# A hybrid decoder layer: projection evacuations at the recurrent chain's rank, and attention tiles taken narrow and wide by turns

## The chip, the cores and the metric

The kernel runs on one core of one Trainium2 chip. Each engine (TensorE or PE, VectorE or DVE, ScalarE or ACT, GpSimd or POOL, SyncE or SP) works through its own queue in order; semaphores order work between them. The metric is device time in microseconds (us) for one execution of the whole layer. Times are given for the median of several runs; the profile shows one execution of its own.

## The reference

The layer has a model width of 1024 and a sequence of 1024 tokens, batch 1, all float32. It computes two mixers side by side from one input projection, then an MLP:

```python
h = _rms_norm(x, norm_mix_pre[i])
z = h @ w_in_first                       # one combined projection
q, k, v = z[..., 0:512], z[..., 512:1024], z[..., 1024:1536]
zs = _token_shift(z[..., 1536:...], mu_shift[i])   # z + (prev - z) * mu
r_r, k_r, v_r = zs[..., 0:512], zs[..., 512:1024], zs[..., 1024:1536]
attn = _rms_norm(_dilated_attention(q, k, v), attn_out_gain[i])
rw = _rwkv7(r_r, k_r, v_r, xw, xa, xg, ...)        # a recurrence over the tokens
x = x + _rms_norm(jnp.concatenate([attn, rw], -1) @ w_out[i], norm_mix_post[i])
h = _rms_norm(x, norm_ffn_pre[i])
x = x + _rms_norm(jnp.square(jax.nn.relu(h @ w_ffn_up[i])) @ w_ffn_down[i], norm_ffn_post[i])
```

The attention has 8 heads of 64. It is causal, with three dilated branches combined by their softmax denominators; this is the same as one softmax over all earlier keys with the logarithm of a count (how many branches contain the distance) added to the score. The other mixer, RWKV-7, has 8 heads of 64 and a 64x64 state per head, updated token by token.

## The kernel before

**Stages.** Until about 47 us the input is loaded, normalised and transposed, and the first low-rank (LoRA) columns are projected. From 47 to 477 us TensorE does 24 projections of 128 columns each, named `k0`..`k3`, `r0`..`r3`, `v0`..`v3` (for RWKV, one for each pair of heads) and `aq0`..`av3` (queries, keys, values of the attention). Between them it does the RWKV work: for each pair of heads a preparation (`pre_pair`: products `kk`, `ar`, `bk`, `km`, and a matrix `pN`), a triangular inversion on VectorE (`subst`: many small `tmp`, `Zt` steps), its merge (`merge`: `X`, `Z`, `qu`), and then, from about 320 to 455 us, a serial chain over eight blocks of 128 tokens. From 477 to 626 us the attention runs, then the mixing with `w_out` until about 717 us, then the MLP until the end at 1346 us.

**A projection.** It takes two halves of 512 tokens, each in one PSUM bank of the tag `z` (two banks). Each half is 8 steps of three matmuls (a product of split operands in fp32r). After the last step `ev` (in `proj_spill`) evacuates the bank. For RWKV columns that is `shift_evac`: ScalarE writes the bank times 1 − mu (line 198), VectorE keeps the last column times mu as a carry (200) or adds that carry (202), and adds the bank shifted by one token times mu (203). For `aq` and `ak` ScalarE writes a rounded copy and VectorE the remainder, and both go to DRAM (`qk_d`); for `av` ScalarE copies and stores to `zs_d`. Only when the evacuation has read the bank can the next half but one start in it.

**What sets the order.** The queues of TensorE and SP are written out by hand: `drive` interleaves the steps of the projections and of the RWKV jobs by a simulated clock (a job's step yields its cost; due times come from a table), and from the attention on TensorE's order is the order of the code. VectorE, ScalarE and GpSimd are ordered by a scheduler with priorities: `tc.high_priority(offset=n)` lets what is written inside go earlier by n places than where it stands. `PRI = (300, 600, 3500, 2500)`: the preparation and its norms run at 300, `subst`, `merge` and parts of the chain's blocks at 600, the serial steps of the chain at 3500, the attention at 2500. The projections' steps have no such offset.

**The attention.** It runs over 4 pairs of heads, 8 query tiles i of 128 tokens and 2 heads h, 64 steps m in all. A tile i has 128(i+1) keys, so tiles 0 to 3 fit one bank of 512 (narrow here) and 4 to 7 need two (wide). For each step, `at_s` does the scores `pS` (two matmuls for each bank), VectorE adds the penalty strip `stripT` and takes the minimum (894), and ScalarE takes the exp and its sum (896). `at_t` transposes the exps on TensorE into PSUM (`pT`, 906): the first four blocks into bank `a`, copied out by ScalarE (908), the others into bank `c`, copied out by VectorE (910), both into the tile `PT`. `at_s` runs two steps ahead of `at_t`. `at_v` multiplies with the values (`po`) after every second tile. After tiles 3 and 7 it divides (`ao`, 928), stores to `a_d`, squares on ScalarE (`sqa`, 933) and reduces on VectorE (`sq`, 934). `at_vt` transposes the next pair's values (`vt`, 875 and `Vt`, 876). `load_wo` prepares parts of `w_out` (`WO`, 945, 946) without an offset.

**The start of the attention.** SP's queue issues the loads of `qs`, `kh`, `kl` (865), of the values `vT` (870) and of `stripT` (853), in an order that follows from the scheduled program.

Of the kernel before, what the change touches and what calls it, by code (L numbers as in the profile page):

```python
# [8 lines left out]
F32 = mybir.dt.float32  # L9
# [8 lines left out]
P = 128  # L18
# [22 lines left out]
def hybrid_kernel(tc, x, par, cst, strip, win, wup_lora, gup, gnwb, grow, wout, wup, wdown, out, dbg=None):  # L41
# [7 lines left out]
    def mm_h(o, lhsT, rhs, start=True, stop=True):  # L49

        for s_ in range(2):
            last = mm(o[64 * s_:64 * s_ + 64], lhsT[:, 64 * s_:64 * s_ + 64], rhs, start, stop)
        return last
# [10 lines left out]
    with (  # L64
# [658 lines left out]
        def slabs(todo, done):  # L723

            def pick():
                j = next((j for j, t in enumerate(todo) if t[3] is None or t[3] in done), None)
                if j is None:
                    return None
                u = todo.pop(j)
                raw, hi_, lo_ = load_w(wslab(2 + u[1]), u[0], A)  # L730
                for q in (slice(0, 4), slice(4, 8)):
                    V.tensor_tensor(lo_[:, q], raw[:, q], hi_[:, q].bitcast(F32), OP.subtract)
                return u, hi_, lo_

            nxt = None
            while todo or nxt:
                nxt = nxt or pick()
                if not nxt:
                    yield None
                    continue  # L740
                (nm, i, shift, _), hi_, lo_ = nxt
                nxt = pick()
                ev = proj_spill(nm, i, shift)
                for hf in range(2):
                    pz = ps.tile([P, 512], F32, name=f"z_{nm}_{hf}", tag="z")
                    ts = slice(hf * 512, hf * 512 + 512)
                    for k in range(KB):
                        mm3(pz, hi_[:, k, :], lo_[:, k, :], hT[:, 0, k, ts], hT[:, 1, k, ts], k == 0, k == KB - 1)
                        if k == KB - 1:
                            ev(hf, pz)  # L750
                        yield 0.7, [f"{nm}_{hf}", nm][:1 + hf] if k == KB - 1 else []

        def drive(todo, jobs):
# [99 lines left out]
        nc.sync.dma_start(stripT, strip)  # L853

        at, sx, pts, pos, aset = {}, {}, {}, {}, {0: ap_}

        def at_load(p):

# [19 lines left out]
        def at_s(p, i, h):  # L878

            QS, KH, KL = at[p]  # L880
            w = P * (i + 1)
            if i == 0 and h == 0:
                at[p, "den"] = sm.tile([P, 8, 2], F32, name=f"den{p}", tag="den")
                at[p, "rden"] = sm.tile([P, 8, 2], F32, name=f"rden{p}", tag="rden")
            Sx = sx[p, i, h] = ap_.tile([P, S], F32, name=f"S{p}_{i}_{h}", tag="Sx", bufs=3)
            mn = sm.tile([P, 2], F32, name=f"mn{p}_{i}_{h}", tag="mn", bufs=4)
            nbk = 1 if w <= 512 else 2
            for k in range(nbk):
                lo, hi = 512 * k, min(w, 512 * k + 512)
                pS = ps.tile([P, 512], F32, name=f"pS{p}_{i}_{h}_{k}", tag="wz"[k if i > 3 else h] if p > 0 or i > 4 else "w")  # L890
                for q in range(2):
                    mm(pS[:, :hi - lo], QS[h][:, i * P:(i + 1) * P], (KH, KL)[q][h][:, lo:hi], q == 0, q == 1)
                so = S - w + lo
                V.tensor_tensor_reduce(Sx[:, lo:hi], pS[:, :hi - lo], stripT[:, so:so + hi - lo], 1.0,  # L894
                                       3e38 if k == 0 else mn[:, 0:1], OP.add, OP.min, accum_out=mn[:, k:k + 1])
            A.activation(Sx[:, :w], Sx[:, :w], AF.Exp, scale=-1.0, bias=mn[:, nbk - 1:nbk], accum_out=at[p, "den"][:, i, h:h + 1])  # L896
# [14 lines left out]

        def at_v(p, i0):

            Vt, qg = at[p, "v"], i0 // 4
            if i0 % 4 == 0:
                pos[p, qg] = ps.tile([P, 4, 2, 64], F32, name=f"po{p}_{qg}", tag="by"[qg], bufs=1)
            po = pos[p, qg]
            for i in (i0, i0 + 1):
                for h in range(2):
                    PT = pts.pop((p, i, h))  # L920
                    for j in range(i + 1):
                        mm_h(po[:, i % 4, h], PT[:, j], Vt[:, j, h * 64:h * 64 + 64], j == 0, j == i)
            if i0 % 4 == 0:
                return
            rden = at[p, "rden"][:, 4 * qg:4 * qg + 4]
            V.reciprocal(rden, at[p, "den"][:, 4 * qg:4 * qg + 4])
            ao = ap_.tile([P, 4, 2, 64], F32, name=f"ao{p}_{qg}", tag="ao", bufs=1)
# [153 lines left out]
        for _ in range(LEAD):  # L1081
            next(rest, None)
        hi_pri = lambda: tc.high_priority(offset=PRI[3])
        step = lambda m: (m // 16, m % 16 // 2, m % 2)
        with hi_pri():
            at_load(0)
            at_s(*step(0))
            at_s(*step(1))
        for m in range(64):
            p, i, h = step(m)  # L1090
            with hi_pri():
                if m + 2 < 64:
                    at_s(*step(m + 2))
                at_t(p, i, h)
                if h == 1 and i % 2 == 0 and m > 1:
                    at_v(*((p, i - 2) if i else (p - 1, 6)))
                if h == 1 and i == 0:
                    at_vt(p)
                if m == 17 or m == 33:
                    at_load(p + 1)  # L1100
# [411 lines left out]
```

## Time and profile before

| | us |
|---|---|
| median of 3 runs | 1355.21 |
| lowest and highest run | 1354.86, 1359.75 |
| the profiled execution's own time | 1348.41 |
| its span in the profile | 1346.3 |
| VectorE busy | 903.5 |
| ScalarE busy | 624.8 |

The profiled execution is 6.8 us below the median of the runs. The span leaves out 2.1 us around the first and last instruction. A row of waits gives the engine and the line that waited, then who released it, the sum in us, how often, and the longest. A row of a timeline gives the start in us, the duration of one, the engine, the line, the operation, its output and inputs, and in brackets how long the engine had stood and who released it. In such rows names have lost their numbers: `z_v` is any half of any of the `v` projections. A window's row gives its bounds, its length, busy time and count of PE, weight loads, DVE, ACT and POOL, the clock granted to TensorE (1.00 is full), the DMA engines' busy share and GB/s.

### The profile page before, as it was taken

The page shows a single profiled execution, that of the slowest core. Times are in us where ns is not written, and L with a number is a line of the kernel's source. Part 1 is how long each engine was busy: PE and PEld are TensorE (multiplying, and loading weights), DVE is VectorE, ACT ScalarE, POOL GpSimd, SP SyncE. Part 2 cuts the span into 40 slices and gives each one's busy share as a digit, 9 for nine tenths or more (in the row PEclk, how much of TensorE's full clock was granted, in tenths as well). Part 3 has the DMA queues.
Part 4 walks back from the last instruction along what each step waited for, and adds up shares of the span by engine and source line. Part 5 has one row for each costly group of instructions (what it writes and reads, how often), then busy time and mean ns, then how long its engine had stood idle before and what let it go on. Part 6 is the DMA issues. An engine that isn't in the chain of part 4 may idle for free.

```text
span 1346.3 us, 23565 instructions
## 1 busy us (share of the span) xinstructions
PE 1280.9 (95%) x9360; PEld 1056.4 (78%) x9360; DVE 903.5 (67%) x1647; ACT 624.8 (46%) x1026; POOL 36.2 (3%) x56
## 2 busy tenths in 40 slices
PE   6999999899999988999998999999999999999997
PEld 5777888787777867787886788888888888888875
DVE  7867657632678556555889977667766776456587
ACT  7652324223455366665647444343444344443442
POOL 0000000000000000000000000000000002000210
PEclk9999999999999999999999999999999999999999
DMA  7346746778686587602434454454467985345564
GB/s 257 115 172 165 196 119 187 196 217 240 168 255 190 168 271 186 168 17 87 139 112 141 164 168 137 157 172 148 138 199 232 344 332 160 105 135 194 188 206 168
DMA packets 163757, 239.48 MB, mean 178 GB/s; under 512 B 52192, under 2 KB 89312, under 8 KB 163648
## 3 DMA queue, kind: packets, MB, share of 16 engines
q1 hardware_dynamic: 154304, 212.81, 50.5%
q10 hardware_dynamic: 8064, 20.98, 4.7%
q0 software_dynamic: 1280, 4.20, 0.8%
q8 instruction: 73, 1.20, 0.4%
q14 instruction: 36, 0.29, 0.1%
HBM read 160.85 MB, written 77.09 MB: 177 GB/s over the span
## 4 chain that ended last, share of the span: by engine, by line
PE 72%; DVE 12%; DMA 8%; ACT 4%; issue 3%; SPq 1%; DVEq 0%; ACTq 0%
PE X L47 12%; PE dX L47 9%; PE Z L47 6%; PE pm L47 6%; PE dZ L47 5%; PE dY L47 3%; PE z_v L47 3%; PE z_aq L47 3%; PE Y L47 3%; PE z_k L47 3%; DMA bv<-v_d 2%; PE po L47 2%; PE pT L906 2%; PE z_av L47 2%; PE z_r L47 2%
## 5 line engine op out<-in xcount | busy, mean ns | idle before, releaser
L47 PE MATMUL dX<-wow,wou 128*128 128x512 f32 x768 | 175.9, 390 | 2.4 <-DVE wow L1173 1.9
L47 PEld LDWEIGHTS dX<-wow,wou 128*128 128x128 f32 x768 | 143.8, 188 | 33.8 <-DVE wow L1173 3.2
L47 PE MATMUL dZ<-wow,wou 128*128 128x512 f32 x384 | 87.4, 389 | 0.0
L47 PEld LDWEIGHTS dZ<-wow,wou 128*128 128x128 f32 x384 | 72.1, 188 | 15.0
L1172 ACT ACTIVATE wow<-wd 128x1024 fp32r<-128x1024 f32 x40 | 42.3, 1060 | 88.6 <-PE dZ L47 29.8
L1173 DVE TENSOR_TENSOR wou<-ur,wou 128x1024 fp32r<-128x1024 f32 x56 | 72.0, 1287 | 7.3 <-ACT wou L1172 7.1
L1173 DVE TENSOR_TENSOR wow<-wd,wow 128x1024 fp32r<-128x1024 f32 x40 | 49.9, 1250 | 34.5 <-ACT wow L1172 33.9
L1172 ACT ACTIVATE wou<-ur 128x1024 fp32r<-128x1024 f32 x56 | 58.5, 1048 | 20.7 <-DMA ur<-u_d 13.3
L894 DVE CUSTOM_DVE_ANT_0 S<-pS,stripT 128x512 f32<-128x512 f32 (+3 forms) x64 | 37.5, 588 | 33.9 <-PE pS L47 19.5
L896 ACT ACTIVATE S<-S,mn 128x128 f32<-128x128 f32 (+7 forms) x64 | 49.4, 772 | 17.3 <-DVE mn L894 17.1
L1260 ACT ACTIVATE r<-u 128x512 f32<-128x512 f32 x48 | 30.0, 626 | 52.1 <-DVE u L1258 51.9
L906 PE MATMUL pT<-cst,S 128*128 128x128 f32 x288 | 44.7, 279 | 8.7 <-DVE PT L910 4.2
L47 PE MATMUL z_aq<-hT,wh_aq 128*128 128x512 f32 x128 | 47.3, 424 | 3.5 <-DVE ev_v L203 3.5
L47 PE MATMUL pm<-WO,mxr 128*128 128x512 f32 x192 | 49.4, 400 | 1.0 <-DVE mn L894 0.7
L1173 DVE TENSOR_TENSOR wow<-TK,wow 128x1024 fp32r<-128x1024 f32 x16 | 20.8, 1301 | 38.9 <-ACT wow L1172 38.9
L906 PEld LDWEIGHTS pT<-cst,S 128*128 128x128 f32 x288 | 32.3, 140 | 17.9 <-ACT PT L908 6.7
L47 PE MATMUL Z<-HB,wo 128*128 128x512 f32 x192 | 46.1, 389 | 0.0
L47 PE MATMUL pm<-WO,mxa 128*128 128x512 f32 x192 | 45.8, 394 | 0.0
L47 PE MATMUL z_k<-hT,wh_k 128*128 128x512 f32 x128 | 44.0, 405 | 1.7 <-DVE z L234 1.4
L47 PE MATMUL z_av<-hT,wh_av 128*128 128x512 f32 x128 | 45.3, 408 | 0.0
L47 PE MATMUL X<-HB,wo 128*128 128x512 f32 x180 | 43.7, 390 | 1.6 <-ACT HB L1034 1.6
L47 PE MATMUL z_v<-hT,wh_v 128*128 128x512 f32 x128 | 42.9, 400 | 1.0 <-DVE ev_r L203 1.0
(388 smaller groups left out, 3056.1 us busy)
## 6 DMA issues: line engine op xcount, KB each, us to landing
ur<-u_d SPq DMA_DIRECT2D x56, 512.0 KB, 4.4
wd<-in_wdown_dram SPq DMA_DIRECT2D x40, 512.0 KB, 4.2
u_d<-S SPq DMA_DIRECT2D x64, 256.0 KB, 2.1
u_d<-u SPq DMA_DIRECT2D x48, 256.0 KB, 2.2
wr_upa<-in_wup_dram SPq DMA_DIRECT2D x16, 512.0 KB, 3.6
wr_upb<-in_wup_dram SPq DMA_DIRECT2D x16, 512.0 KB, 4.0
TK<-in_wdown_dram SPq DMA_DIRECT2D x16, 512.0 KB, 7.4
x<-in_x_dram SPq DMA_DIRECT2D x8, 512.0 KB, 6.9
```

Source lines behind the costliest of these rows:

```text
L47: return PE.matmul(o, lhsT, rhs, start=start, stop=stop, skip_group_check=True)
L894: V.tensor_tensor_reduce(Sx[:, lo:hi], pS[:, :hi - lo], stripT[:, so:so + hi - lo], 1.0, 3e38 if k == 0 else mn[:, 0:1], OP.add, OP.min, a ...
L896: A.activation(Sx[:, :w], Sx[:, :w], AF.Exp, scale=-1.0, bias=mn[:, nbk - 1:nbk], accum_out=at[p, "den"][:, i, h:h + 1])
L906: PE.transpose(pt[:, j], Sx[:, (4 * k + j) * P:(4 * k + j + 1) * P], ident)
L1172: A.activation(w[:, 0, 0:n], raw, AF.Copy)
L1173: E.tensor_tensor(w[:, 1, 0:n], raw, w[:, 0, 0:n].bitcast(F32), OP.subtract)
L1260: A.activation(r, src, AF.Relu)
```

## The change

The change has three parts. First, the evacuation of each projection is written inside the offset `PRI[2]`, 3500, that of the chain's serial steps. Second, the attention takes its query tiles in the order `TO`, 0, 4, 1, 5, 2, 6, 3, 7, so that a narrow and a wide tile come by turns. With it, the scores of a narrow tile always use banks of the tag `w`, and of a wide tile `w` and `z`; before, the second head's narrow tiles used `z`. In pair 0 the first five tiles of the new order use `w` alone, since the last projection still holds `z`. Third, both `po` banks are taken at a pair's start, and division, store and square move into `at_out`, called for both halves at the end of a pair. The line numbers after the change differ by 1 before the attention and by 2 to 4 in it.

```diff
--- before.py
+++ after.py
@@ -747,7 +747,8 @@
                     for k in range(KB):
                         mm3(pz, hi_[:, k, :], lo_[:, k, :], hT[:, 0, k, ts], hT[:, 1, k, ts], k == 0, k == KB - 1)
                         if k == KB - 1:
-                            ev(hf, pz)
+                            with tc.high_priority(offset=PRI[2]):
+                                ev(hf, pz)
                         yield 0.7, [f"{nm}_{hf}", nm][:1 + hf] if k == KB - 1 else []
@@ -853,6 +854,7 @@
         at, sx, pts, pos, aset = {}, {}, {}, {}, {0: ap_}
+        TO = [0, 4, 1, 5, 2, 6, 3, 7]
@@ -879,7 +881,7 @@
-            if i == 0 and h == 0:
+            if (p, "den") not in at:
@@ -887,7 +889,7 @@
-                pS = ps.tile([P, 512], F32, name=f"pS{p}_{i}_{h}_{k}", tag="wz"[k if i > 3 else h] if p > 0 or i > 4 else "w")
+                pS = ps.tile([P, 512], F32, name=f"pS{p}_{i}_{h}_{k}", tag="wz"[k] if p > 0 or TO.index(i) > 4 else "w")
@@ -911,17 +913,19 @@
         def at_v(p, i0):
 
-            Vt, qg = at[p, "v"], i0 // 4
-            if i0 % 4 == 0:
-                pos[p, qg] = ps.tile([P, 4, 2, 64], F32, name=f"po{p}_{qg}", tag="by"[qg], bufs=1)
-            po = pos[p, qg]
-            for i in (i0, i0 + 1):
+            Vt = at[p, "v"]
+            if i0 == 0:
+                pos[p] = [ps.tile([P, 4, 2, 64], F32, name=f"po{p}_{qg}", tag="by"[qg], bufs=1) for qg in range(2)]
+            for i in TO[i0:i0 + 2]:
                 for h in range(2):
                     PT = pts.pop((p, i, h))
                     for j in range(i + 1):
-                        mm_h(po[:, i % 4, h], PT[:, j], Vt[:, j, h * 64:h * 64 + 64], j == 0, j == i)
-            if i0 % 4 == 0:
-                return
+                        mm_h(pos[p][i // 4][:, i % 4, h], PT[:, j], Vt[:, j, h * 64:h * 64 + 64], j == 0, j == i)
+                if i0 == 6:
+                    at_out(p, i // 4)
+
+        def at_out(p, qg):
+            po = pos[p][qg]
             rden = at[p, "rden"][:, 4 * qg:4 * qg + 4]
...
@@ -1081,17 +1085,18 @@
-        step = lambda m: (m // 16, m % 16 // 2, m % 2)
+        step = lambda m: (m // 16, TO[m % 16 // 2], m % 2)
...
         for m in range(64):
-            p, i, h = step(m)
+            p, h = m // 16, m % 2
+            i = m % 16 // 2
             with hi_pri():
                 if m + 2 < 64:
                     at_s(*step(m + 2))
-                at_t(p, i, h)
+                at_t(*step(m))
```

What moves on the engines is shown at three places; in these rows a name has lost the number of its pair, and the number behind the last underscore is only an identity.

VectorE at the preparation of pair 3 (around 229 us before). `car_v` and `ev_v_0` are the evacuation of the first half of `v3`, `ev_v_1` that of the second; `ar`, `kk`, `bk`, `km` belong to the preparation, `wl_ak` is a weight's remainder.

```order
 L430 TENSOR_TENSOR ar_1_2499<-kk_1_2497,P_1_2443 128x8x64
+L200 TENSOR_SCALAR car_v_2393<-z_v_0_2294,par 128x1
+L203 SCALAR_TENSOR_TENSOR ev_v_0_2392<-z_v_0_2294,par,ev_v_0_2392 128x511
 L431 SCALAR_TENSOR_TENSOR kk_0_2447<-in_0_2048,kk_0_2447 128x512
 L431 SCALAR_TENSOR_TENSOR kk_1_2497<-in_1_2049,kk_1_2497 128x512
...
-L200 TENSOR_SCALAR car_v_2393<-z_v_0_2294,par 128x1
+L732 TENSOR_TENSOR wl_ak_2477<-wr_ak_2474,wh_ak_2476 128x512
 L450 SCALAR_TENSOR_TENSOR ev_r_1_1889<-ev_r_1_1889,par,km_1_2562 128x512
 L451 TENSOR_TENSOR bk_1_2500<-km_1_2562,in_1_2049 128x8x64
-L203 SCALAR_TENSOR_TENSOR ev_v_0_2392<-z_v_0_2294,par,ev_v_0_2392 128x511
```

The first half's evacuation moved from behind the last `bk` to a place ahead of the two `kk`.

VectorE at the preparation of pair 1 (around 124 us before). `ev_v_1` is the evacuation of the second half of `v0`; `bk_1` is what the second half of `pN` needs.

```order
+L202 TENSOR_TENSOR ev_v_1_1239<-ev_v_1_1239,car_v_1210 128x1
+L203 SCALAR_TENSOR_TENSOR ev_v_1_1239<-z_v_1_1214,par,ev_v_1_1239 128x511
+L491 TENSOR_REDUCE Zt_1100<-tmp_1105 128x8x8
 L431 SCALAR_TENSOR_TENSOR kk_0_1267<-in_0_1163,kk_0_1267 128x512
-L491 TENSOR_REDUCE Zt_1100<-tmp_1105 128x8x8
+L430 TENSOR_TENSOR ar_1_1315<-kk_1_1313,P_1_1263 128x8x64
 L432 TENSOR_TENSOR bk_0_1270<-kk_0_1267,in_0_1163 128x8x64
-L430 TENSOR_TENSOR ar_1_1315<-kk_1_1313,P_1_1263 128x8x64
+L431 SCALAR_TENSOR_TENSOR kk_1_1313<-in_1_1164,kk_1_1313 128x512
 L446 TENSOR_TENSOR ar_0_1269<-ev_r_0_1038,P_0_1259 128x8x64
-L431 SCALAR_TENSOR_TENSOR kk_1_1313<-in_1_1164,kk_1_1313 128x512
+L432 TENSOR_TENSOR bk_1_1316<-kk_1_1313,in_1_1164 128x8x64
```

The evacuation and one `ar` now stand ahead of the first `bk`.

ScalarE in pair 0 of the attention, first the rows before, then those of the change. `S_i_h` is the exp of tile i and head h, `PT_i_h` the copy of its transposes from bank `a`, `ev_av_1` the last projection's evacuation, `WO` a part of `w_out`.

```order
381 L896 ACTIVATE S_3_1_5313,den_5208<-S_3_1_5313,mn_3_1_5314 128x512
382 L713 ACTIVATE ev_av_1_5342<-z_av_1_5183 128x512
383 L945 ACTIVATE WO_6346<-wo_6344,par 128x1024
384 L908 ACTIVATE PT_3_0_5356<-pT_3_0_0_5357 128x512
385 L896 ACTIVATE S_4_0_5345,den_5208<-S_4_0_5345,mn_4_0_5346 128x640
386 L908 ACTIVATE PT_3_1_5374<-pT_3_1_0_5375 128x512
```

```order
381 L898 ACTIVATE S_5_1_5334,den_5208<-S_5_1_5334,mn_5_1_5335 128x768
382 L713 ACTIVATE ev_av_1_5379<-z_av_1_5183 128x512
383 L949 ACTIVATE WO_6383<-wo_6381,par 128x1024
384 L719 DMA zs_d<-ev_av_1_5379 128x512
385 L898 ACTIVATE S_2_0_5382,den_5208<-S_2_0_5382,mn_2_0_5383 128x384
386 L898 ACTIVATE S_2_1_5400,den_5208<-S_2_1_5400,mn_2_1_5401 128x384
387 L910 ACTIVATE PT_5_0_5389<-pT_5_0_0_5390 128x512
388 L949 ACTIVATE WO_6799<-wo_6797,par 128x1024
```

Between `WO` and the next copy from bank `a` there are now two exps; before there was none.

## The prediction

> **What bounds the kernel now.** The page comes first.
>
> ```profile
> span 1346.3 us, 23565 instructions
> PE 1280.9 (95%) x9360; PEld 1056.4 (78%) x9360; DVE 903.5 (67%) x1647; ACT 624.8 (46%) x1026; POOL 36.2 (3%) x56
> PE 72%; DVE 12%; DMA 8%; ACT 4%; issue 3%; SPq 1%; DVEq 0%; ACTq 0%
> ```
>
> TensorE works 95% of the span and carries 72% of the chain that ended last. The change takes no matmul away. It can only win the time in which TensorE stands, and the rest of the program has to pass that time on. So the second view is the list of TensorE's waits, over the two places that the change touches: the stretch of the projections before the chain's own part (75 to 260 us), then the attention by pairs of heads (each pair takes some 35 us).
>
> ```profile
> PE z_aq L47 <- DVE ev_v L203: 3.5, 1, 3.5
> PE pN L47 <- DVE bk L432: 2.9, 1, 2.9
> PE z_v L47 <- DVE ev_r L203: 1.0, 1, 1.0
> PE z_k L47 <- ACT ev_k L198: 0.3, 1, 0.3
> ```
>
> Columns: who waits for whom, us in total, times, longest. Three of these four are waits of a projection for its PSUM bank, which an evacuation (`ev_`) has not yet read out: 4.8 us. The second is the reverse: TensorE waits for a product of the chain's preparation, `bk`, and the change puts evacuations ahead of just such products.
>
> For the attention, first the start (476 to 484), then pair 0 (484 to 520), pair 1 (520 to 555), pair 2 (555 to 590), pair 3 (590 to 626):
>
> ```profile
> PE pS L47 <- DMA kl<-qk_d: 1.5, 1, 1.5
> PE pS L47 <- DVE mn L894: 1.4, 1, 1.4
> ...
> PE pT L906 <- DVE PT L910: 1.2, 2, 0.7
> PE pS L47 <- DVE mn L894: 0.9, 2, 0.8
> PE pT L906 <- ACT PT L908: 0.6, 2, 0.4
> ...
> PE pT L906 <- DVE PT L910: 1.5, 1, 1.5
> PE pT L906 <- ACT Vt L876: 0.9, 1, 0.9
> PE pT L906 <- ACT PT L908: 0.8, 2, 0.6
> ...
> PE pT L906 <- ACT Vt L876: 0.9, 1, 0.9
> PE pm L47 <- DVE mn L894: 0.7, 1, 0.7
> ...
> PE pT L906 <- DVE PT L910: 1.5, 1, 1.5
> ```
>
> The start stands 2.9 us. Pair 0 stands 3.1 (0.4 of it in a row left out), pair 1 3.2, pair 2 1.6, pair 3 1.5, and with the rows of 0.4 and less that are left out some 9.8 us in all, most of it because a bank of transposed scores (`pT`) has not been copied out. That is the most that the new attention order can win.
>
> **The projections, part by part.** No instruction is added; evacuations move up in VectorE's and ScalarE's queues, TensorE's own order stays. The large wait, at `z_aq`:
>
> ```profile
> 229.18 1.28 DVE L431 SCALAR_TENSOR_TENSOR kk<-in,kk 128x512 f32<-128x512 f32 x2
> ...
> 238.11 0.74 DVE L203 SCALAR_TENSOR_TENSOR ev_v<-z_v,par,ev_v 128x511 f32<-128x511 f32 x1
> ...
> 238.84 0.74 DVE L203 SCALAR_TENSOR_TENSOR ev_v<-z_v,par,ev_v 128x511 f32<-128x511 f32 x1
> 239.00 0.64 PE L47 MATMUL z_aq<-hT,wh_aq 128*128 128x512 f32 x1 [3.54 <-DVE ev_v L203]
> ```
>
> TensorE arrives at 239.00 − 3.54 = 235.46. In the new order the first half's evacuation stands right before the two `kk` of 229.18, so its bank is free by 229.2 + 0.74 = 230, five microseconds early; the second half follows behind one `ar` and lies ahead of its bank's next user too. The stall goes whole: **+3.5**. What is late next is the chain's preparation behind it (0.9 us of queue), which has slack, since TensorE now has `z_aq`'s matmuls to do meanwhile.
>
> The stall cost more than itself. A window's row gives each engine's busy time and, behind POOL's, the granted clock:
>
> ```profile
> 126.50:129.90 3.40, 3.40 (x10) 2.72 (x9) 3.40 (x7) 0.00 (x0) 0.58 (x3) 0.50 0.15 18
> 239.20:242.50 3.30, 3.30 (x9) 2.52 (x9) 2.73 (x4) 0.00 (x0) 0.00 (x0) 0.50 0.19 35
> 358.70:362.00 3.30, 1.51 (x38) 1.30 (x38) 1.87 (x3) 2.59 (x5) 0.00 (x0) 1.00 1.09 314
> 362.10:365.40 3.30, 3.30 (x21) 2.35 (x16) 1.81 (x6) 0.59 (x1) 0.00 (x0) 0.50 0.99 176
> 539.00:542.40 3.40, 3.40 (x23) 2.73 (x22) 2.59 (x7) 3.19 (x6) 0.00 (x0) 1.00 0.58 205
> ```
>
> After the 3.54 us at 239 the clock stood at 0.50 for about 3.4 us, which delays the work by half of it: without the stall another **+1.7**. The same follows the 2.93 us at 125, which stays.
>
> The wait at `z_v`:
>
> ```profile
> 187.75 0.21 DVE L200 TENSOR_SCALAR car_r<-z_r,par 128x1 f32<-128x1 f32 x1
> 188.80 0.74 DVE L203 SCALAR_TENSOR_TENSOR ev_r<-z_r,par,ev_r 128x511 f32<-128x511 f32 x1
> ```
>
> The evacuation moves ahead of six or more of the preparation's instructions of 0.6 to 0.7 us, several us earlier; the 1.0 us stall goes: **+1.0**. The 0.3 at `z_k` goes too (its ScalarE half moves up): **+0.3**.
>
> Now the price, at `pN`:
>
> ```profile
> 124.01 0.70 DVE L491 TENSOR_REDUCE Zt<-tmp 128x64 f32<-128x512 f32 x1
> 124.61 0.70 DVE L432 TENSOR_TENSOR bk<-kk,in 128x512 f32<-128x512 f32 x1
> 125.36 1.15 PE L47 MATMUL pN<-ar,bk 64*64 64x64 f32 x32 [2.93 <-DVE bk L432]
> ```
>
> VectorE works without a pause here, and successive starts lie 0.60 apart. The new order puts the evacuation of `ev_v0`'s second half (with its carry 0.73, by the start-to-start distance of the two rows at 238) and one `ar` (0.60) ahead of this `bk`: 1.3 us later, and TensorE is waiting already: **−1.3**, with 4.2 us of stall where 2.9 were. The bounds: −0.7 if only the evacuation counts, −2.0 if a second `ar` slips ahead. In the LoRA stretch before (59 to 70 us) evacuations pass the `tl` copies on ScalarE; I cost it at nothing, since a longer wait there is followed by one that VectorE sets; without that cover it would be one evacuation on ScalarE, 0.6 (the copies of 128x512 below took 0.59).
>
> Projections: 3.5 + 1.7 + 1.0 + 0.3 − 1.3 = **+5.2** (bounds +3.5 and +6.2).
>
> **The start of the attention.** The strip of penalties is asked for behind `kl`, whose wait ends at 473.30:
>
> ```profile
> 473.30 1.08 SPq L865 DMA_DIRECT2D kl<-qk_d  x2
> 474.43 0.59 SPq L853 DMA_DIRECT2D stripT<-in_strip_dram  x1
> ```
>
> In the new order `vT`, 512 KB like the strip, which went out ahead of both before, is issued between these two rows, and the first score's evacuation waits for the strip. The bounds: nothing, if `kl` alone sets the start, and 1.7 if the strip must wait for all of `vT`'s bytes (512 KB at the 314 GB/s of the window at 358.7). I take **−0.6**, one more issue like the strip's own (0.59), since `vT` needs no more than that of the queue itself.
>
> **The attention.** Scores, exps, transposes and copies are the same in number; their order and banks differ. (i) `ao`, its square and the reduction no longer fall in the middle of a pair. The 1.5 us stall of pair 1 shows what they did:
>
> ```profile
> 534.44 0.69 DVE L928 TENSOR_TENSOR ao<-po,rden 128x512 f32<-128x512 f32 x1 [1.10 <-PE po L47]
> 535.83 0.69 DVE L934 TENSOR_REDUCE sq<-sqa 128x4 f32<-128x512 f32 x1
> 538.26 0.42 DVE L910 COPY PT<-pT 128x256 f32<-128x256 f32 x1
> ```
>
> 0.69 + 0.69 us of VectorE stand ahead of scores and copies that TensorE needs by 537.3. Pairs 1 and 3 have that stall in the middle; by the new order it goes in both: +1.5 each. (ii) At a pair's hand-over now both halves' `ao` come at once, so the next pair's first copies stand behind two `ao`, two squares on ScalarE and two reductions. I walked TensorE's new order by hand with the rows' durations: pair 1 loses about 0.8 there (a copy behind the second square and a score), pair 2 0.4. The end of pair 3 adds 0.3 of tail. (iii) Pair 0: ScalarE's queue now reads evacuation, WO, two exps of 384, then the copy of tile 5.
>
> ```profile
> 493.62 1.14 ACT L945 ACTIVATE WO<-wo,par 128x1024 fp32r<-128x1024 f32 x1
> L908 ACT ACTIVATE PT<-pT 128x512 f32<-128x512 f32 x40 | 23.6, 589 | 11.0 <-PE pT L906 10.7
> L896 ACT ACTIVATE S<-S,mn 128x384 f32<-128x384 f32 x8 | 4.9, 613 | 0.5 <-DVE mn L894 0.4
> ```
>
> WO 1.14 + two exps of 0.61 with their reads + the copy 0.59: the copy ends about 499.9, and TensorE wants its bank at about 497.65: a new stall of 2.2, where the old order let a copy go between WO and the next exp. With 1.4 of small waits that stay, pair 0 stands 3.6 instead of 3.1: −0.5. Sum: 1.5 + 1.5 − 0.8 − 0.4 − 0.5 = **+1.3**, tail counted inside the rounding of pair 3. Bounds: +9.8 if each wait goes, and −8.0 in the slow rival below.
>
> Total: 5.2 + 1.3 − 0.6 = 5.9. The profiled execution took 1348.4, 6.8 us below the median of the runs, 1355.2; its like after the change comes to 1348.4 − 5.9 = 1342.5, and on the scale of the median 1355.2 − 5.9 = **1349.3**, −0.44%. About 0.5%, 6.8 us, is what a measurement of this kernel can tell from no change.
>
> **Rivals.**
> *The new stall halves the clock.* In the rows above 1.79 us of standing within 3.3 (358.7 to 362) were followed by a stretch at 0.50, while the stall of 1.5 us in pair 1, which ended at 538.8, was not (539.0 to 542.4 at 1.00). Pair 0's new 2.2 us is longer than either. One such stretch costs 1.7: gain 4.2, **1351.0**. The Trainium skill ("TensorE: Matmul & The Clock Gate", section "Part 1: The HAM clock gate (the "warmup" mystery)") lets the clock fall only when the array idled through a whole free-running window, stated as 4096 cycles or 3.4 us. By that rule 2.2 us would cost nothing and the forecast stands; the row at 358.7, half idle, speaks against reading it so strictly, the one at 239 agrees.
> *The attention's waits all go.* Alternating tiles leave a narrow tile's time for each wide copy. 5.2 − 0.6 + 9.8 = 14.4: **1340.8**. For it: nearly all waits there are for `pT`'s banks, each under 1.6. Against: Vt's waits (0.9) sit at the hand-over, which the new order burdens.
> *The gain is swallowed.* TensorE arrives 5 us earlier at the chain's merges, and if a transfer or VectorE sets their end, as at `pN`, TensorE stands there instead. Then the projections' part is lost but for the half clock, 1.7: **1353.5**. For it: VectorE had no pause in the rows at 124 and 229 to 239. Against: the waits of 75 to 260 show no other one of weight between the three.
> *Slower: ScalarE's queue in pair 0.* Three WO conversions lie in it. If each stands ahead of a copy that TensorE awaits, 3 × 2.2 = 6.6 of stall, two stretches at half clock 3.4, and the strip at its upper bound, 1.1 more than counted: 11.1, against 3.1 of old stalls, 8.0 lost. With pairs 1 to 3 winning nothing, 5.2 − 0.6 − 8.0 = −3.4: **1358.6**. It decides once pair 0 stands 4.6 + 3.1 = 7.7 us. For it: the second and third WO stand ahead of copies in the new queue. Against: these copies are of a tile whose bank TensorE needs later, and the old order had the same WO there.
>
> **How the numbers follow.** Chances: forecast (gain 3 to 9) 0.45; half clock 0.13; all waits go 0.12; swallowed 0.18; slower 0.12. The forecast's centre is just short of 0.5%, so a little under half of it, 0.2, counts as faster; all of 14.4 us (0.12) and 0.05 of the half-clock case, whose other terms may be larger, join it: faster 0.37. Slower 0.09 from the last rival, the rest of which is too small to see. Same 0.54. The likeliest case's own range is 1346 to 1352. Cutting nearly nothing off the case at 1340.8 and the better part of the slow one, the range is 1341.0 to 1357.0.
>
> **What would show it.** Right: no wait of `z_aq` or `z_v` for an `ev_`, clock 1.00 where `z_aq` starts, `pN`'s wait at about 4.2, no wait over 1 us for VectorE's PT in the middle of pairs 1 and 3, one of about 2.2 for ScalarE's PT in pair 0, and a first score some 0.6 later after its projections end. Wrong: a new wait of TensorE between 240 and 470 as long as what was won; waits at the hand-overs over 2 us; more stretches at 0.50 than the three that stay (125, 362, 481); or the strip coming more than 1 us late.

## The result, and the profile after

The changed kernel took 1345.35 us in the median of 6 runs (1343.01 to 1350.0), the kernel before 1355.03 in the runs beside them. The ratio is 0.9938, 95% interval 0.9918 to 0.9958: faster by 0.6%, or 8 us. A second series gave 0.9945 (0.9929 to 0.9961). The ratios are the ones on record and not quotients of the medians, which lie 9.7 and 7.9 us apart in the two series. The forecast was 1349.3 in a range of 1341.0 to 1357.0; the time lies inside, on the better side.

The profiled execution took 1343.01 us. The page of the changed kernel:

```profile
span 1340.9 us, 23552 instructions
PE 1278.6 (95%) x9360; PEld 1057.0 (79%) x9360; DVE 904.7 (67%) x1647; ACT 625.3 (47%) x1026; POOL 36.1 (3%) x56
PE 76%; DVE 10%; DMA 8%; ACT 4%; issue 2%; SPq 0%; DVEq 0%; ACTq 0%
```

The work is the same, and the span is 5.4 us shorter (1346.3 before); VectorE's share of the chain that ended last fell from 12% to 10%. The waits of TensorE, first in the stretch of the projections (75 to 260 us), then by pieces of the attention: its start (468 to 475), pair 0 (475 to 511), pair 1 (511 to 542), pair 2 (542 to 576), pair 3 (576 to 612) and the passage to the mixing (612 to 628):

```profile
PE pN L47 <- DVE bk L432: 4.2, 1, 4.2
...
PE pS L47 <- DVE mn L896: 2.5, 1, 2.5
PE pS L47 <- DMA kl<-qk_d: 1.2, 1, 1.2
...
PE pT L908 <- ACT PT L910: 2.3, 2, 2.0
PE pT L908 <- ACT Vt L878: 1.3, 1, 1.3
...
PE pT L908 <- ACT PT L910: 1.0, 3, 0.4
PE pT L908 <- DVE PT L912: 0.6, 1, 0.6
PE pT L908 <- ACT Vt L878: 0.5, 1, 0.5
...
PE pm L47 <- DVE mxr L976: 0.8, 1, 0.8
PE pT L908 <- ACT Vt L878: 0.5, 1, 0.5
PE pT L908 <- ACT PT L910: 0.3, 1, 0.3
...
PE pT L908 <- ACT PT L910: 1.7, 1, 1.7
...
PE mxta L973 <- ACT ma L987: 1.8, 1, 1.8
PE mxta L973 <- DVE mxa L976: 1.5, 1, 1.5
```

The three waits for evacuations are gone, the wait of `pN` has grown to 4.2, the waits of 1.5 for VectorE's PT in the middle of pairs 1 and 3 are gone. New are 2.0 in pair 0, 1.3 for the copy `Vt` at its start, 1.7 at the start of pair 3 and 1.8 at the passage.

Where TensorE stands against the kernel before is read from the starts of the same work in both timelines:

| TensorE's start of | before | after | difference |
|---|---|---|---|
| `z_aq`, first matmul | 239.00 | 234.24 | −4.8 |
| first score of the attention | 477.06 | 468.07 | −9.0 |
| last `pm` from the RWKV half, after the last `po` | 625.49 | 614.23 | −11.3 |
| third group of `mxta`, behind the first long `pm` from the attention half | 639.22 | 631.49 | −7.7 |
| end of the span | 1346.3 | 1340.9 | −5.4 |

The lead of 9.0 us comes from the projections and the chain, the attention adds 2.3, the passage to the mixing gives 3.6 back, and what follows, the MLP above all, another 2.3. The 2.3 of the attention are not in the list of waits: from the first score to the passage it sums to 12.8 us in both profiles. Gaps of under 0.15 us account for some 0.7 of them, and the matmuls' own time for the rest; why is not shown. Three windows of the changed kernel belong to these steps:

```profile
239.20:242.50 3.30, 3.30 (x41) 2.58 (x42) 3.21 (x6) 0.60 (x1) 0.00 (x0) 1.00 0.38 99
470.40:477.20 6.80, 4.62 (x15) 3.95 (x16) 2.14 (x9) 3.04 (x9) 0.00 (x0) 0.50 0.91 367
624.00:627.40 3.40, 3.40 (x11) 2.81 (x12) 0.69 (x1) 1.21 (x2) 0.00 (x0) 0.50 0.47 126
```

The clock is full where it stood at 0.50 before (239), and half at the passage (624), where it was full. At the attention's start the half clock lasted 6.8 us, twice as long as before; TensorE worked for 4.6 us of it, against 3.0 in the 3.4 us of before, so some 0.8 us more were lost there.

The passage's wait itself shows on VectorE:

```profile
612.48 0.69 DVE L932 TENSOR_TENSOR ao<-po,rden 128x512 f32<-128x512 f32 x1 [0.18 <-PE po L47]
613.87 0.69 DVE L938 TENSOR_REDUCE sq<-sqa 128x4 f32<-128x512 f32 x1 [0.70 <-ACT sqa L937]
616.17 0.69 DVE L932 TENSOR_TENSOR ao<-po,rden 128x512 f32<-128x512 f32 x1 [1.61 <-DMA a_d<-ao]
617.62 0.69 DVE L938 TENSOR_REDUCE sq<-sqa 128x4 f32<-128x512 f32 x1 [0.76 <-ACT sqa L937]
```

The second `ao` is not waiting for its sums (TensorE's last `po` ended at 614.3) but for the store of the first one, since the tile `ao` has a single buffer. Behind it come the reduction, the root for the attention's norm, `ma` on ScalarE and only then the first `mxta`. The same thing stands at pair 3's start, on VectorE and then on ScalarE:

```profile
583.94 0.69 DVE L932 TENSOR_TENSOR ao<-po,rden 128x512 f32<-128x512 f32 x1 [2.68 <-DMA a_d<-ao]
...
584.73 0.63 ACT L937 ACTIVATE sqa<-ao 128x512 f32<-128x512 f32 x1 [2.24 <-DVE ao L932]
585.26 0.58 ACT L910 ACTIVATE PT<-pT 128x512 f32<-128x512 f32 x1
```

VectorE stood 2.7 us with that `ao` at its queue's head, ScalarE 2.2 us for its square, and the copy of PT that TensorE needed was queued behind the square.

### The profile page after: what moved, and what is told of

The parts are those of the page before. It is cut to its first block, busy times and chain, and to the rows that moved or that the text cites. A ratio compares the mean times of both kernels' runs of the same rounds, so it can differ in the third digit from the quotient of the medians.

```text
span 1340.9 us, 23552 instructions
## 1 busy us (share of the span) xinstructions
PE 1278.6 (95%) x9360; PEld 1057.0 (79%) x9360; DVE 904.7 (67%) x1647; ACT 625.3 (47%) x1026; POOL 36.1 (3%) x56
## 4 chain that ended last, share of the span: by engine, by line
PE 76%; DVE 10%; DMA 8%; ACT 4%; issue 2%; SPq 0%; DVEq 0%; ACTq 0%
PE X L47 12%; PE dX L47 8%; PE Z L47 6%; PE pm L47 5%; PE dZ L47 5%; PE z_aq L47 3%; PE dY L47 3%; PE z_v L47 3%; PE z_k L47 3%; PE z_av L47 3%; PE Y L47 3%; PE z_ak L47 3%; PE z_r L47 3%; DMA wd<-in_wdown_dram 2%; PE pS L47 2%; PE pT L908 2%
## 5 line engine op out<-in xcount | busy, mean ns | idle before, releaser
L47 PE MATMUL dY<-wow,wou 128*128 128x512 f32 x192 | 43.7, 389 | 0.0
```

The source lines that it names most:

```text
L47: return PE.matmul(o, lhsT, rhs, start=start, stop=stop, skip_group_check=True)
```

## The experiments

All are timed against the kernel before on the same chip (1353.4 to 1353.8 us there; the table's first two rows are from the first series), on three chips; the last column sums TensorE's waits of over 0.15 us in one profile of each, first in the 14 us from the attention's first score, then inside, from there to the passage, then in the 6 us of the passage. The ratio is again the one on record: the quotient of the medians can differ from it by a thousandth.

| kernel | median us | ratio to before | 95% interval | start / inside / passage, us of waits |
|---|---|---|---|---|
| before | 1355.0 | 1 | | 3.3 / 9.5 / 1.4 |
| the change | 1345.4 | 0.9938 | 0.9918 to 0.9958 | 5.0 / 7.8 / 3.3 |
| the change again | 1345.6 | 0.9945 | 0.9929 to 0.9961 | 3.9 / 7.3 / 3.1 |
| rank only | 1347.6 | 0.9947 | 0.9927 to 0.9966 | 3.8 / 11.0 / 1.4 |
| attention only | 1351.0 | 0.9978 | 0.9957 to 0.9999 | 4.3 / 7.1 / 2.8 |
| v3 unranked | 1349.6 | 0.9971 | 0.9951 to 0.9992 | 4.8 / 5.6 / 3.5 |
| v0's second half unranked | 1343.6 | 0.9924 | 0.9896 to 0.9953 | 3.7 / 5.6 / 3.0 |
| score banks as before | 1343.7 | 0.9933 | 0.9915 to 0.9952 | 4.9 / 7.6 / 2.8 |
| conversions of `w_out` held | 1345.6 | 0.9944 | 0.9923 to 0.9966 | 5.0 / 9.3 / 2.9 |
| `ao` in two buffers | 1344.0 | 0.9916 | 0.9886 to 0.9947 | 5.7 / 7.7 / 1.4 |
| strip first | 1340.9 | 0.9909 | 0.9878 to 0.9940 | 4.2 / 7.2 / 2.9 |
| three mends | 1338.5 | 0.9887 | 0.9864 to 0.9910 | 3.8 / 7.9 / 1.9 |
| old order, mended | 1346.3 | 0.9951 | 0.9936 to 0.9965 | 6.3 / 11.0 / 1.4 |

### Each half of the change alone

The kernel before with the first hunk of the diff:

```diff
                         if k == KB - 1:
-                            ev(hf, pz)
+                            with tc.high_priority(offset=PRI[2]):
+                                ev(hf, pz)
```

> The kernel before with the first part of the change alone: evacuations at the chain's rank, attention as before. My theory, that the rank brings the gain: TensorE reaches the end of the chain 8 to 9 us earlier than in the kernel before, as after the whole change (8.96), the waits of z_aq and z_v are gone and pN's is 4.2; the attention then costs what it cost before, and what it returned to the mixing after the whole change (3.6 us) is not lost. So 6.5 to 8.5 us faster than before, as fast as the whole change or a little faster. Rival, that the new attention order brings a good part: at most 4 us faster than before, because what the projections won comes back as a wait at the attention's start.

And the change without that hunk:

> The change without its first part: evacuations as before, attention in the new order. My theory: the stalls of 3.5 and 1.0 us at z_aq and z_v are back, pN's is 2.9; inside the attention 2 us are won, 0.8 lost at its start and 3 lost at its end, where the first mixing tile waits for ao of the second half: between 1 us faster and 2 us slower than before. Rival, that the attention order brings a good part: 4 to 5 us faster than before.

Rank alone gave 0.9947, which is 7.2 us (4.6 to 9.9). The rival's bound of 4 us is excluded; the rank is the larger part. One step of that theory did not show in the profile: TensorE came to the first score at 472.47, 4.6 us earlier than before and not 8 to 9. Over the nine other profiles with the rank (that with v3 unranked left out) that start lies between 465.9 and 473.9, so the 9.0 of the change's first profile is one value of a wide spread. Attention alone gave 0.9978, 3.0 us (0.1 to 5.8): more than my theory's upper end of 1, less than the rival's 4 to 5, and its interval reaches both. Added up, the two ratios make 0.9925; the whole change has 0.9938 and 0.9945, so on top of the rank the new attention order is worth little that these runs can tell.

The waits say how that comes. Here is TensorE's list inside the attention, first of the kernel with the rank only (486.5 to 628.5), then of the one with the new attention only (494.7 to 632):

```profile
PE pT L907 <- DVE PT L911: 4.9, 4, 1.5
PE pT L907 <- ACT PT L909: 3.0, 5, 1.0
PE pT L907 <- ACT Vt L877: 2.0, 3, 0.9
PE pm L47 <- DVE mn L895: 0.7, 1, 0.7
```

```profile
PE pT L907 <- ACT PT L909: 5.3, 7, 2.0
PE pT L907 <- ACT Vt L877: 1.0, 2, 0.5
PE pm L47 <- DVE mxr L975: 0.8, 1, 0.8
```

The waits for VectorE's copies (4.9) go altogether, and those for ScalarE's grow from 3.0 to 5.3. By the table, the old order waits 9.5 to 11.0 inside, the new one, unmended, 5.6 to 7.8; but it pays 1.4 to 2.1 more at the passage in each profile, and up to 1.7 at the start. Whole stretches say the same. From the first score to TensorE's arrival at the passage, the three kernels with the old order took 154.1 to 158.4 us, the ten with the new one 149.8 to 152.3. Up to the third group of `mxta`, behind the passage, it was 162.2 to 166.5 against 159.9 to 163.4: the gain inside is real, and part of it is paid back at the passage.

### The evacuation that freed z_aq's bank

One value projection goes back to its old rank:

```diff
-                            with tc.high_priority(offset=PRI[2]):
+                            with tc.high_priority(offset=0 if i == 11 else PRI[2]):
                                 ev(hf, pz)
```

> The whole change, but the evacuations of the last value projection (v3, both halves) keep the rank they had before. Theory: TensorE's wait at z_aq comes back at 3.5 us, with the stretch at half clock behind it (1.7 more), and the first row of z_aq slips by about 3.5 against the whole change: 4 to 5.5 us slower than the whole change, which is most of what the rank brought. Rival, that z_aq's wait was cover for something that is late anyway: the wait comes back and the chain's end stays where it was, under 1.5 us slower.

The ratio rises from 0.9938 or 0.9945 to 0.9971: about 4 us are gone, as the theory said, though the intervals just overlap. The list of waits (75 to 260), and the window behind the second one:

```profile
PE pN L47 <- DVE bk L432: 4.2, 1, 4.2
PE z_aq L47 <- DVE ev_v L203: 3.5, 1, 3.5
...
240.30:243.70 3.40, 3.40 (x9) 2.64 (x9) 1.52 (x2) 0.00 (x0) 0.00 (x0) 0.50 0.48 154
```

The place of one projection's evacuations carries about half of what the rank brought, and a stretch at half clock comes with it. The first score starts at 475.60, against 468.07 and 472.34 in the two profiles of the change: the delay is not taken up before the chain's end. The rival, that the wait had been cover for something late anyway, falls.

### The price at pN

The second half of `v0` goes back instead (`i == 8 and hf` in the line above).

> The whole change, but the evacuation of the second half of v0 keeps the rank it had before. Theory: VectorE's bk comes 1.3 us earlier, TensorE's wait at pN falls from 4.2 to 2.9, the stretch at half clock stays, z_k2 does not wait over 0.3: the chain's end 1.0 to 1.3 us earlier, 1 us faster than the whole change. Rival, that v0's evacuation is then late for its bank's next user: pN's wait falls, but a wait of z_k2 for ev_v over 0.5 us takes its place and nothing is won.

The waits (75 to 260), and the window behind `pN`'s wait, which answers to that of 126.50 in the kernel before:

```profile
PE pN L47 <- DVE bk L432: 2.9, 1, 2.9
PE z_k L47 <- ACT ev_k L198: 0.3, 1, 0.3
...
125.60:129.00 3.40, 3.40 (x43) 2.88 (x42) 3.40 (x7) 0.00 (x0) 0.12 (x1) 1.00 0.36 43
```

The wait falls from 4.2 to 2.9, as forecast, and nothing but 0.3 of `z_k` takes its place. In this profile the clock also stayed full behind it. `z_aq` starts at 232.91, 1.3 us earlier than in the change's earlier profile; but the first score, at 472.40, is not earlier than there (468.07 and 472.34), so the forecast for the chain's end did not come true in this profile. The time, 0.9924, is 1.5 to 2.1 thousandths below the change's, 2 to 3 us, with overlapping intervals. The shorter wait is shown; that the kernel is faster is not.

### The buffer of ao

```diff
-            ao = ap_.tile([P, 4, 2, 64], F32, name=f"ao{p}_{qg}", tag="ao", bufs=1)
+            ao = ap_.tile([P, 4, 2, 64], F32, name=f"ao{p}_{qg}", tag="ao", bufs=2)
```

> The whole change, with two buffers for the tile ao instead of one. Theory: at the end of each pair the second half's ao waits on VectorE until the first half's store has left the only buffer (at the last pair: ao at 616.17, though its sums were ready at 614.30), and copies and scores queue behind it. Then with two buffers ao follows within 0.3 us of its sums, the first mixing tile's wait falls from 1.8 to about 0, the wait of 1.7 for ScalarE's PT at pair 3's start falls below 0.5, and the kernel is 3 to 5 us faster than the whole change. Rival, that the wait is the work of the two ao, squares and reductions itself and not the buffer: the waits stay within 0.5 us of what they were and the time within 1 us.

VectorE at the passage, and TensorE's waits from 580 to 592 (pair 3's start) and from 612 to 630 (the passage):

```profile
618.40 0.69 DVE L938 TENSOR_REDUCE sq<-sqa 128x4 f32<-128x512 f32 x1 [0.69 <-ACT sqa L937]
619.00 0.68 DVE L932 TENSOR_TENSOR ao<-po,rden 128x512 f32<-128x512 f32 x1
...
PE pT L908 <- ACT Vt L878: 0.4, 1, 0.4
...
PE mxta L973 <- DVE mxa L976: 1.4, 1, 1.4
```

The second `ao` follows the first reduction at once. The wait of 1.8 for `ma` is gone, pair 3's 1.7 has become 0.4, and the passage waits 1.4 as in the kernel before. The buffer was the cause, not the work of the two `ao`. But inside the attention the waits sum to 7.7 as in the change (7.8): at the starts of pairs 1 and 2 TensorE now waits 1.3 each for the copy `Vt`, where it was 0.5. What this profile shows as won is the passage, 1.9. In time that is 0.9916, 3 to 4 us below the two series of the change by the ratios and 1.4 to 1.6 by the medians, with overlapping intervals.

### The start of the attention

```diff
-        nc.sync.dma_start(stripT, strip)
+        with tc.high_priority(offset=PRI[3]):
+            nc.sync.dma_start(stripT, strip)
```

> The whole change, with the penalty strip's load put ahead of the loads of qs, kh, kl and vT on SP's queue. Theory: the second wait at the attention's start (2.5 us for the first score's minimum) is the strip, which lands at 472.1 because it is issued behind kl and vT; it goes, the wait for kl (1.2) stays or grows by up to 0.7, and the kernel is 1.5 to 2.5 us faster than the whole change. Rival, that the wait moves on to kl, whose data are late anyway: the start stands as long as before in sum (3.8 us) and the time stays within 0.7 us.

In the change, VectorE's first score waits for the strip (first row); with the strip first, TensorE's waits at the start (468 to 478) are one row:

```profile
472.22 0.29 DVE L896 CUSTOM_DVE_ANT_0 S<-pS,stripT 128x128 f32<-128x128 f32 x1 [9.43 <-DMA stripT<-in_strip_dram]
```

```profile
PE pS L47 <- DMA kl<-qk_d: 2.8, 1, 2.8
```

The strip's wait of 2.5 is gone, and 1.6 of it has moved to `kl` (1.2 before the mend): 1 us is won at this place. In time the kernel came out at 0.9909, 4 to 5 us below the change, which is more than this place accounts for. Theory and rival each had a part, and the rest I cannot place.

### Pair 0's new wait

The conversions of the attention's part of `w_out` on ScalarE, three of which stood in pair 0, are held behind pair 0's last copy:

```diff
-                    A.activation(PT[:, 0:nb_], pt[:, 0:nb_], AF.Copy)
+                    lastc = A.activation(PT[:, 0:nb_], pt[:, 0:nb_], AF.Copy)
+                    if (p, i, h) == (0, 7, 1):
+                        at["hold"] = lastc
...
-                A.activation(w[:, 0], raw, AF.Copy, scale=ga)
+                with tc.issue_after(at["hold"].ins):
+                    A.activation(w[:, 0], raw, AF.Copy, scale=ga)
```

> The whole change, with the first three conversions of w_out on ScalarE (1.14 us each) held back until the last copy of pair 0. Theory: pair 0's wait of 2.0 us for ScalarE's PT came from the conversion between ev_av and two exps; without it the wait is 0.9 to 1.1, the conversions land at the start of pair 1 and lengthen the waits there by less than 0.5: about 0.7 us faster than the whole change. Rival, that the two exps alone make the wait: it stays above 1.7.

TensorE's waits from 488 to 632 in this kernel:

```profile
PE pT L908 <- ACT PT L910: 6.1, 8, 1.1
...
PE pT L908 <- ACT Vt L878: 1.3, 2, 0.8
PE pS L47 <- DMA kl<-qk_d: 1.1, 1, 1.1
```

Pair 0's wait fell from 2.0 to 1.0, as it must if the conversion stood in it. But the whole list did not get shorter (9.3 inside, 7.8 in the change): three waits for ScalarE's copies in pairs 1 and 2 grew to between 0.8 and 1.1, where the change has 0.3 to 0.4, and a load of `kl` came 1.1 late. The time is that of the change, 0.9944. The cause of the wait is shown; that holding the conversions back like this pays is not, and why the later waits grew stays open.

### The score banks

```diff
-                pS = ps.tile([P, 512], F32, name=f"pS{p}_{i}_{h}_{k}", tag="wz"[k] if p > 0 or TO.index(i) > 4 else "w")
+                pS = ps.tile([P, 512], F32, name=f"pS{p}_{i}_{h}_{k}", tag="wz"[k if i > 3 else h] if p > 0 or TO.index(i) > 4 else "w")
```

> The whole change, but a narrow tile's second head takes its score bank from the tag z again, as before the change; instructions and their order on each engine are those of the whole change. Theory: the banks are not what the new order lives on: waits of the attention within 1 us of the whole change's (8.1 inside it), time within 2 us. Rival, that a narrow tile in z meets a wide tile's second block there: waits of pS for mn appear inside the pairs, 2 us or more in sum.

0.9933, waits inside of 7.6, and none of `pS` for `mn` inside the pairs: the banks make no difference that shows.

### What the order is worth once mended

Three of the mends together (two buffers for `ao`, the strip first, `v0`'s second half at its old rank):

> The whole change with three mends together: two buffers for ao, the strip's load first, v0's second half at its old rank. Theory: they act at different places and add up, pN's wait 2.9, no wait for the strip, no wait over 0.5 at pair 3's start and none of the first mixing tile for ScalarE's ma: 5 to 8 us faster than the whole change, 1.0 to 1.2% faster than before. Rival, that what is won is lost again at the next wait for kl and in the mixing: under 3 us faster than the whole change.

And the old attention order with the mends that apply to it: the rank, but not for `v0`'s second half, and the strip first.

> The kernel before with the rank (v0's second half left out) and the strip's load first, attention in the old order with its one buffer for ao: against the whole change with three mends it tells what the new attention order is worth once its losses are mended. Theory: waits inside the attention are 10 to 12 us as in the two other kernels with the old order, against 8.1 with the new one, start and tail alike: 2 to 4 us slower than the whole change with three mends. Rival, that the order is worth nothing and the mends are all: within 1 us of it.

The three mends reach 0.9887 (0.9864 to 0.9910), 1338.5 us: 1.1% faster than the kernel before and some 7 us faster than the change. That is inside the forecast of 5 to 8, though by the ratios the three alone promised some 9 to 12. The old order with its mends stays at 0.9951. That is 8.7 us more, and only part of it is the order: inside the attention it waits 11.0 against 7.9, 3.1 more, as the theory said. Another 2.5 come from the start (6.3 against 3.8; rank only, without the strip's edit, has 3.8 too), as the waits of that kernel from 466 to 477 show:

```profile
PE pS L47 <- DMA kl<-qk_d: 5.6, 1, 5.6
```

In that kernel `kl`'s second load is issued at 466.99, right behind `vT`; with the strip first in the new order it goes ahead of `vT`, at 466.72. Whether this made it late is not shown. So the run's time does not isolate the order; the stretches and waits inside the attention are the better measure. The passage costs the old order 0.5 less, so 3 to 4 us remain that I did not place.

### The change once more

> The changed kernel itself once more, to stand beside the two others on one chip: 0.993 to 0.995 of the kernel before; its wait at pN 4.2, no wait of z_aq or z_v for an evacuation. Whether pair 0's wait of 2.0 us is followed by a stretch at half clock is open: in three of seven profiles with that wait it was.

0.9945, as expected. `pN` waited 4.6, not 4.2; no evacuation was waited for, and pair 0's wait of 2.0 was followed by a stretch at half clock.

## Why the prediction was right, and where it was not

The sum was made against one profile: 5.9 us forecast there, 5.4 measured between the two profiles. That these agree is partly luck. TensorE's lead at the first score was forecast as 5.2 and came to 9.0; the start and the attention were to add 0.7 and added 2.3; what followed was to cost nothing beyond 0.3 of tail and cost 5.9. Over the runs the change won 7 to 8 us by the ratios. The granted clock shows a part of that difference: the kernel before had 0.993 in its profile but 0.988 to 0.989 in the mean of its other runs, that is, its profile had few of the half-clock stretches that its runs have; the change's mean is 0.989 to 0.990.

- **z_aq, +3.5 and +1.7**: right in place, size and mechanism. Without v3's rank the wait of 3.5 and the half clock came back, and 4 us of time with them.
- **z_v +1.0 and z_k +0.3**: both waits are gone from the list.
- **The projections' sum, +5.2**: the lead at 250 us was 6.3, above the stated upper bound of 6.2 as well. The 1.1 more are 0.65 that TensorE already had when it came to `pN` (121.78 against 122.43) and some 0.5 behind that wait. The LoRA stretch cost nothing, as counted: the lead behind it, at 70 us, was 0.0. The bound of 6.2 does not follow from the terms given; with 0.7 for `pN` they make 5.8.
- **pN, −1.3**: the wait is 4.2, as forecast. It grew because the evacuation and one `ar` went ahead of `bk`, as the prediction said. Taking the stretch at half clock behind it as given was too mild: all 8 profiles with a wait of 4.2 or more had a stretch there, four of them a double one, while with 2.9 it was 3 of 5.
- **The strip, −0.6**: the two waits of the start summed to 2.9 before and 3.8 after, −0.8. The cause was as named: the strip is what the first score waited for. The longer stretch at half clock behind these waits, some 0.8 more, was not in the sum.
- **Pair 0, −0.5**: 3.6 us of waits forecast, 3.6 measured, 2.0 of it where the forecast put 2.2. The conversion stood in it, as the run that held it shows. The times 499.9 and 497.65 from which the 2.2 was taken follow from no row shown: counted from 493.62 the terms named end at about 496.7. And the rest agrees by luck: of the 1.4 of small waits that were to stay, 0.3 did, and 1.3 is a new wait for `Vt`.
- **Pairs 1 and 2**: 2.1 and 1.6 measured, about 2.5 and 2.0 forecast.
- **The end of pair 3 and of the attention**: here the step failed that read "The end of pair 3 adds 0.3 of tail", and with it the one that left pair 3 with next to no wait. Two `ao` in a row share one buffer, so the second waits for a store, 1.6 us at the passage and 2.7 at pair 3's start, with the queues of VectorE and ScalarE behind it. The passage cost 1.9 more than before (1.8 + 1.5 against 1.4) and a half-clock stretch, 1.7; pair 3 waited 1.7 where 0.2 was left. The two-buffer run shows the cause. I had counted the instructions that move and not the time for which the moved store holds its buffer.
- **What covered it up**: the chain itself. TensorE's lead grew by 2.7 us between 320 us and the chain's end, which was not forecast, since its waits at `O` and `E` there were shorter. The two largest, before and then after:

```profile
PE O L47 <- DVE HV L642: 3.3, 2, 2.1
PE O L47 <- DMA T<-ar_d: 1.9, 2, 1.3
...
PE O L47 <- DVE HV L642: 1.9, 2, 1.7
PE O L47 <- DMA T<-ar_d: 1.0, 1, 1.0
```

Whether the rank causes this stays open: all waits from 320 us to the first score sum to between 5.8 and 8.5 us in the eleven profiles with the rank, 8.8 and 9.4 in the two without, which fits but varies widely.
- **The loss of 2.3 at the end** was not forecast. The longest wait for `wow` there is 1.1 us before and 2.3 after; it is 0.6 to 2.3 over all profiles, of kernels that do not differ there. From the third group of `mxta` to the end the thirteen profiles take 706.6 to 711.3 us (707.1 before, 709.4 after), so the 2.3 lies inside the spread between executions.

Of the rivals, the slow one did not come, since the second and third conversion made no wait. "The gain is swallowed" is refuted by the v3 run; its time of 1353.5 left out the 0.7 of the start and the attention, with which it would be 1352.8. "All waits go" fails at the waits for ScalarE, which grew. The half-clock rival is real but not in the first profile of the change: pair 0's wait of 2.0 was followed by a stretch in 4 of 9 profiles. One of the named signs of being wrong did appear there: a fourth stretch at half clock, the one at the passage.

## What to carry to other kernels

An evacuation holds a bank that the busiest engine will want; on a list-scheduled engine its rank decides a stall on that engine, and one such place was worth about 4 us, while the same edit at another place cost 1.3 of waiting: rank them one by one. When an output step is moved to where two of its kind follow each other, count the buffers and the stores, not only the instructions: a single-buffered tile made VectorE wait for a DMA and stopped two queues. A new order of work is worth judging after its hand-overs are mended, since before that part of its gain inside was paid back at the passage.

## What the runs showed of the hardware

Waits of the same length are sometimes followed by a stretch at half clock and sometimes not. Over 13 profiles: 4 of 9 after pair 0's 2.0 us, 3 of 5 after `pN`'s 2.9, 3 of 3 after `z_aq`'s 3.5, 8 of 8 after `pN`'s 4.2 to 4.6. One such case is the attention-only kernel, where pair 0's 2.04 us ended at 504.2; beside it stands the same wait in the change, which ended at 491.8:

```profile
504.50:507.90 3.40, 3.40 (x15) 3.01 (x14) 1.75 (x5) 1.86 (x3) 0.00 (x0) 0.50 1.06 289
```

```profile
492.00:495.40 3.40, 3.35 (x26) 2.53 (x26) 2.70 (x5) 2.76 (x5) 0.00 (x0) 1.00 1.06 268
```

Each stretch but the one at a profile's very end lasts 3.413 us or twice that, and costs about half its length while TensorE works: behind `z_aq` the lead grew from 4.8 to 6.3 us over the stretch of 3.4 that only the kernel before has. In every profile the starts of its stretches lie whole multiples of 3.413 us apart (125.67, 354.36, 470.41 and 624.01 in the change), so they sit on a fixed grid. The grid explains the chance. In the attention-only kernel the wait fell into one window of the grid; in the change it was divided between two:

```profile
501.11:504.52 3.41, 1.37 (x12) 1.05 (x11) 2.73 (x6) 3.05 (x7) 0.00 (x0) 1.00 0.68 195
```

```profile
487.48:490.89 3.41, 2.28 (x15) 1.77 (x13) 1.96 (x6) 2.90 (x7) 0.00 (x0) 1.00 0.21 32
490.89:494.30 3.41, 2.51 (x16) 2.17 (x17) 2.37 (x4) 3.41 (x7) 0.00 (x0) 1.00 1.06 302
```

TensorE stood 2.04 us of the first window, and 1.13 and 0.90 of the two others. Over the thirteen profiles, from 60 us to the last 8, there are 44 windows of the grid at full clock in which it stood 1.95 us or more, and a stretch follows all 44. Of the 70 with 1.40 to 1.94 it follows 17, and of more than 4600 with less, one. A stretch went on for a second window in 14 of the 15 cases in which TensorE stood 0.52 us or more in its first, and never with less. So a wait is worth more than its length on average, and a single profile can hide or exaggerate that. The Trainium skill ("TensorE: Matmul & The Clock Gate", section "Part 1: The HAM clock gate (the "warmup" mystery)") describes a free-running window of about 3.4 us, and a clock that falls after at least one idle window. A free window fits the chance and the length of 3.413 us seen here. The condition, taken as a whole window without work, does not: waits of 2.0 us, shorter than the window, tripped it.
